# Ten of 544 weight steps with other matmul shapes and orders, and both halves of x in one tile

## The chip, the cores and the metric

The kernel runs on one core of a Trainium2 chip. The metric is the device time of one execution in microseconds, the median over runs. The core has five engines with queues of their own: TensorE (PE in the profile; its weight loads stand apart as PEld), VectorE (DVE), ScalarE (ACT), GpSimd (POOL) and SyncE (SP), which issues nearly all DMAs here.

## The reference

One inference step of a decoder layer on 256 prompt tokens and 8 sample tokens, 264 columns in all:

```
hn = RMSNorm(h);  P = hn @ W_in        # 4096 columns of hn, W_in cut into groups
A: sliding-window attention (12 heads of 128, window 128, sinks, ALiBi), times silu(z_a)
B: mLSTM matrix memory (6 heads), per-head RMS norm, sigmoid gate o_t, times silu(z_m)
C: chunked spatial gating (8 groups), times silu(z_c)
h = h + concat(A, B, C) @ W_out;  then a final RMSNorm
```

The two projections carry nearly all of the arithmetic. Everything is fp32. Beside y the step returns new rows of keys and values and the states of B and C.

## The kernel before

**Steps.** Activations stand transposed: 128 rows of the contraction on the partitions, the 264 tokens along the free axis, so x is 32 tiles k of 128 x 264. The weights are cut into 34 groups g of 512 output columns: 26 for W_in (`GROUPS`), then 8 for W_out (`NGO`). A group is done in 16 steps c, each with two tiles k (`KK = 2`): 34 x 16 = 544 steps (g, c), numbered n. A step's weights are one DMA of 512 KB (`load_w`, tile `wf`, 3 buffers, issued four steps ahead on SyncE's queue).

**Split into two.** Matmuls are in a shortened fp32 type (float32r), and precision comes from a split. For each step ScalarE writes the shortened weights `wh`, and VectorE writes the rest, `wl = wf - wh` (`split_w`, two steps ahead, 3 buffers each). x is split likewise into `xh` and `xl`, two tiles of 128 x 32 x 264 (`split_x` at the start, `split_y` for W_out). Each product is then three matmuls: `wh` with `xh`, `wh` with `xl`, `wl` with `xh`, each 128 x 128 weights by 264 columns.

**Order within a step.** For each of four blocks j of 128 output columns, for both k, the three matmuls go into the same PSUM bank; the four banks `mp` belong to the group. That is 4 x 2 x 3 = 24 matmuls a step, and six in a row into one bank:

```
for j in range(4):
    tick()
    out = main_ps[j][:, :T]
    for kk in range(KK):
        k = KK * c + kk
        s = slice(P * j, P * j + P)
        PE.matmul(out, wh[:, kk, s], xh[:, k], start=(k == 0), stop=False)
        PE.matmul(out, wh[:, kk, s], xl[:, k], start=False, stop=False)
        PE.matmul(out, wl[:, kk, s], xh[:, k], start=False, stop=(k == KT - 1))
    if c == NCH - 1:
        ...
            evac(g, kind, i, out)
```

**End of a group.** After step 15 `evac` empties a bank as soon as its j is done. For groups 8 and 9 (kind `mo`, the output gate of B) VectorE writes `et = mp * rstd`, and ScalarE later takes the sigmoid into `yb`. The next group writes the same four banks, so its first matmul into a bank waits until that bank has been read.

**Other work.** Attention and memory are generators. The recorder keeps a tally of the time that issued work should take (`clk`; 0.113 us for any float32r matmul, whatever its columns), and `tick()`, called before each j, resumes those generators that are due. So their small matmuls (transposes `mx<-sms`, scores `mx<-kT,aq`, products `mx<-pt,vtok`) stand between the blocks j of the weight steps; VectorE's and ScalarE's parts stand between the splits. Group 7 is the last of three for the attention queries, groups 8 to 10 are the gates `mo`; the heads' attention runs beside groups 6 to 8, that of the samples beside 8 and 9.

Every operation is recorded by one helper, so nearly all rows of the profile name its line, L201; tiles tell them apart.

Of the kernel before, what the change touches and what calls it, by code (L numbers as in the profile page):

```python
# [69 lines left out]
LAG = 6.0  # L70
NCH = KT // KK

SM = {}
# [15 lines left out]
def body(tc, xt, wi, wg, wo, sm, kc, vc, c0, wst, w00, bs, cgain, cbias,  # L89
# [3 lines left out]
    with ExitStack() as ctx:  # L93
# [30 lines left out]

        xh = cp.tile([P, KT, T], F32R, name="xh")
        xl = cp.tile([P, KT, T], F32R, name="xl")
        yb = cp.tile([P, KT, T], F32, name="yb")
# [32 lines left out]
        class Eng:  # L160
            """An engine whose issued work is tallied, so that dependent work is issued when due."""

# [95 lines left out]
        def rsqrt(out, x, scale, v, t):  # L258
            """out = (x * scale + EPS) ** -0.5, with one Newton step; v and t are scratch."""
            n = out.shape[0]  # L260
            V.tensor_scalar(v, x, -0.5 * scale, -0.5 * EPS, ALU.mult, ALU.add)
            A.activation(t, x, AF.Sqrt, scale=scale, bias=epsc[:n, 0:1])
            newton(out, v, t)
# [71 lines left out]

# [1 line left out]
        def gate_loads():  # L337
# [90 lines left out]

# [1 line left out]
        def head_loads(h):  # L430
# [150 lines left out]

# [1 line left out]
        def attn_kv(g):  # L583
# [140 lines left out]

# [1 line left out]
        def gmlp_prep():  # L726
# [80 lines left out]

# [1 line left out]
        def gated(kind, i, t):  # L809
# [142 lines left out]

# [1 line left out]
        def drain():  # L954
# [29 lines left out]
        for n, (g, c) in enumerate(steps):  # L984
# [16 lines left out]
            if g == NG and KK * c + KK > S_C:  # L1001
                while ("c", KK * c + KK - 1 - S_C) not in st:
                    tick(True)
            wh, wl = wh_t.pop(n), wl_t.pop(n)
            for j in range(4):
                tick()
                out = main_ps[j][:, :T]
                for kk in range(KK):
                    k = KK * c + kk
                    s = slice(P * j, P * j + P)  # L1010
                    PE.matmul(out, wh[:, kk, s], xh[:, k], start=(k == 0), stop=False)
                    PE.matmul(out, wh[:, kk, s], xl[:, k], start=False, stop=False)
                    PE.matmul(out, wl[:, kk, s], xh[:, k], start=False, stop=(k == KT - 1))
                if c == NCH - 1:
# [149 lines left out]
```

## Time and profile before

| | |
|---|---|
| two timed runs | 1715.74 and 1716.54 us, median 1716.14 |
| profiled execution, first to last instruction | 1715.0 us (no other time of that execution is recorded) |
| TensorE, matmuls | 1682.7 us (98%), 13754 records |
| TensorE, weight loads | 1664.7 us (97%), 13754 records |
| VectorE | 928.2 us (54%) |
| ScalarE | 733.2 us (43%) |
| GpSimd | 125.2 us (7%) |
| share of the chain that ended last | TensorE 94%, VectorE 3% |
| mean granted clock of TensorE | 0.994 |

A row of a group gives count, busy time and the mean of one. Matmuls and weight loads overlap, so their means are longer than the distance from one to the next; that distance is read from starts in the timeline, or from pieces of the chain that hold a count of matmuls.

### The profile page before, as it was taken

Reading aid. Unit: us, or ns where it says so; the run is one execution under the profiler, and the core shown is the slowest. Engines: PE = TensorE matmul, PEld = TensorE weight load, DVE = VectorE, ACT = ScalarE, POOL = GpSimd, SP = SyncE. Lnnn points to the kernel's source line nnn. Section 1 sums busy time; section 2 is a strip of 40 time slices with the busy share of each in tenths; the row PEclk is TensorE's granted clock in tenths of the full one; section 3 lists DMA queues with packets and bytes.
Section 4 is the critical chain, followed back from the end, with each engine's and each line's share of the span. In section 5 each row is a group of like instructions: output and inputs, shape, how many; then the busy total and the mean of one; then the engine's idle time right before and its main releaser. Section 6 shows DMA issues by size and latency. Waiting matters only on the chain.

```text
span 1715.0 us, 32547 instructions
## 1 busy us (share of the span) xinstructions
PE 1682.7 (98%) x13754; PEld 1664.7 (97%) x13754; DVE 928.2 (54%) x1262; ACT 733.2 (43%) x954; POOL 125.2 (7%) x113
## 2 busy tenths in 40 slices
PE   7999999999999999999999999999999999999995
PEld 7899999999999999999999999999999999999995
DVE  8755444555554455555655566444566554444445
ACT  4444433444444334344444444334454443444442
POOL 7300000000000000000101000000100030000002
PEclk9999999999999999999999999999999999999998
DMA  6566668555556666667677767666666666565663
GB/s 225 176 181 175 183 184 264 180 165 155 161 160 176 182 182 176 208 191 237 214 232 220 240 213 221 177 181 184 201 177 216 198 196 190 180 184 177 181 183 145
DMA packets 102178, 328.92 MB, mean 192 GB/s; under 512 B 11090, under 2 KB 24328, under 8 KB 102032
## 3 DMA queue, kind: packets, MB, share of 16 engines
q1 hardware_dynamic: 101072, 326.04, 62.7%
q8 instruction: 107, 1.75, 0.4%
q10 hardware_dynamic: 960, 0.81, 0.1%
q14 instruction: 39, 0.32, 0.1%
HBM read 314.20 MB, written 12.60 MB: 191 GB/s over the span
## 4 chain that ended last, share of the span: by engine, by line
PE 94%; DVE 3%; DMA 1%; issue 1%; ACT 0%; SPq 0%; DVEq 0%; ACTq 0%
PE mp L201 90%; PE mx L201 3%; DVE wl L201 1%; DVE xl L201 1%; DVE yb L201 1%; DMA wf<-wi 1%; DMA wf<-wo 1%; PE sn L201 0%; ACT wh L201 0%; PE gps L201 0%; DVE rstd L201 0%; DVE TM L201 0%; DVE mvs L201 0%; ACT L201 0%; DVE es L201 0%
## 5 line engine op out<-in xcount | busy, mean ns | idle before, releaser
L201 PE MATMUL mp<-xh,wl 128*128 128x264 f32 x4352 | 1240.6, 285 | 12.6 <-DVE wl L201 12.6
L201 PE MATMUL mp<-xh,wh 128*128 128x264 f32 x4352 | 1251.5, 288 | 0.6 <-ACT wh L201 0.6
L201 PE MATMUL mp<-xl,wh 128*128 128x264 f32 x4352 | 1238.2, 285 | 0.0
L201 DVE TENSOR_TENSOR wl<-wf,wh 128x1024 fp32r<-128x1024 f32 (+1 forms) x545 | 695.0, 1278 | 750.8 <-ACT wh L201 746.0
L201 ACT ACTIVATE wh<-wf 128x1024 fp32r<-128x1024 f32 (+1 forms) x545 | 575.0, 1058 | 839.1 <-PE mp L201 734.2
L201 PEld LDWEIGHTS mp<-xh,wl 128*128 128x128 f32 x4352 | 820.6, 189 | 15.2 <-DVE wl L201 15.0
L201 PEld LDWEIGHTS mp<-xh,wh 128*128 128x128 f32 x4352 | 820.7, 189 | 7.2 <-issue 5.0
L201 PEld LDWEIGHTS mp<-xl,wh 128*128 128x128 f32 x4352 | 820.8, 189 | 0.4
L201 POOL TENSOR_TENSOR acc<-acc,es 128x264 f32<-128x264 f32 x29 | 21.9, 754 | 417.1 <-ACT es L201 415.1
L201 POOL TENSOR_SCALAR_AFFINE_SELECT tmp<-bc 128x128 f32<-128x128 f32 x12 | 4.7, 412 | 496.6 <-DMA bc<-gd 496.6
L201 DVE SCALAR_TENSOR_TENSOR xl<-yb,sms,xh 128x264 fp32r<-128x264 f32 x32 | 35.1, 1135 | 1.2 <-ACT xh L201 1.1
L201 ACT ACT_TABLE_LOAD x25 | 32.1, 1283 | 3.4 <-DVE ar L201 2.2
L201 POOL MEMSET pad<- 128x1024 f32 x2 | 1.9, 950 | 406.4 <-PE mx L201 406.4
L201 POOL TENSOR_TENSOR acc<-acc,sq 128x528 f32<-128x528 f32 x15 | 24.0, 1603 | 1.2
L201 ACT ACTIVATE es<-et 128x264 f32<-128x264 f32 x36 | 14.0, 420 | 21.4 <-DVE yb L201 18.1
L201 POOL TENSOR_TENSOR cb<-cb,bc 128x2056 f32<-128x2056 f32 x6 | 21.7, 3616 | 0.0
L201 POOL TENSOR_TENSOR sq<-yb 128x528 f32<-128x528 f32 x15 | 20.6, 1375 | 9.8 <-DMA yb<-xt 9.1
L201 ACT ACTIVATE es<-yb 128x264 f32<-128x264 f32 x33 | 13.6, 412 | 16.3 <-DVE yb L201 16.3
L201 DVE TENSOR_TENSOR et<-mp,rstd 128x264 f32<-128x264 f32 x56 | 20.3, 423 | 0.0
L201 DVE SCALAR_TENSOR_TENSOR cb<-vb,wsk,cb 128x257 f32<-128x257 f32 x48 | 20.1, 480 | 0.0
L201 ACT ACTIVATE bias<-bias,ar 128x128 f32<-128x128 f32 (+1 forms) x24 | 10.7, 448 | 21.4 <-DVE ar L201 21.2
L201 ACT ACTIVATE xh<-yb 128x264 fp32r<-128x264 f32 x32 | 12.1, 412 | 17.7 <-DVE yb L201 17.7
(178 smaller groups left out, 471.6 us busy)
## 6 DMA issues: line engine op xcount, KB each, us to landing
wf<-wi SPq DMA_DIRECT2D x415, 512.0 KB, 3.6
wf<-wo SPq DMA_DIRECT2D x128, 512.0 KB, 3.6
cb<-c SPq DMA_DIRECT2D x12, 514.0 KB
o_cs<-cb SPq DMA_DIRECT2D x12, 514.0 KB, 6.4
vb<-vsd SPq DMA_DIRECT2D x12, 512.0 KB, 5.2
yb<-xt SPq DMA_DIRECT2D x34, 132.0 KB, 3.7
yb<-xt SPq DMA_DIRECT2D x15, 264.0 KB, 5.3
o_y<-yb SPq DMA_DIRECT2D x7, 528.0 KB, 3.1
```

What stands on the lines that cost most here:

```text
L201: return fn(*a, **k)
```

## The change

Nothing is removed from the arithmetic. `xh` and `xl` become two halves of one tile `xx`, in which row k holds `xh` and then `xl`, 264 columns each. Ten steps of groups 7, 8 and 9 are done in other shapes:

- **tail**, steps (7,6) and (7,7): each matmul is cut at column 256, into 256 and 8 columns.
- **halves**, steps (7,10) and (7,11): each is cut at 132.
- **banks**, steps (8,6) to (8,9): the same 24 matmuls, but j is the innermost loop, so each goes to another bank than the one before it. `tick()` is called once ahead of all 24 and four times behind.
- **wide**, steps (9,6) and (9,7): `wh` with 512 columns of a row of `xx` (all of xh and 248 of xl, into all 512 columns of the bank), `wh` with the last 16 columns of xl, `wl` with xh. At the end of group 9 ScalarE copies the bank's columns 264 to 511, VectorE adds them to columns 0 to 247, copies the other 16, and `evac` goes on from there. Both scratch rows, in `acc`, have one buffer.

```
+WIDE = 9
+SHAPES = {(7, 6): "tail", (7, 7): "tail", (7, 10): "halves", (7, 11): "halves", (8, 6): "banks", (8, 7): "banks",
+          (8, 8): "banks", (8, 9): "banks", (WIDE, 6): "wide", (WIDE, 7): "wide"}
...
-        xh = cp.tile([P, KT, T], F32R, name="xh")
-        xl = cp.tile([P, KT, T], F32R, name="xl")
+        xx = cp.tile([P, KT, 2, T], F32R, name="xx")
+        xh, xl = xx[:, :, 0], xx[:, :, 1]
...
             wh, wl = wh_t.pop(n), wl_t.pop(n)
+            shape = SHAPES.get((g, c), "plain")
+            if shape == "banks":
+                tick()
+                for kk in range(KK):
+                    k = KK * c + kk
+                    for w, x in ((wh, xh), (wh, xl), (wl, xh)):
+                        for j in range(4):
+                            PE.matmul(main_ps[j][:, :T], w[:, kk, P * j:P * j + P], x[:, k],
+                                      start=False, stop=False)
             for j in range(4):
                 tick()
                 out = main_ps[j][:, :T]
-                for kk in range(KK):
+                for kk in range(KK if shape != "banks" else 0):
                     k = KK * c + kk
                     s = slice(P * j, P * j + P)
-                    PE.matmul(out, wh[:, kk, s], xh[:, k], start=(k == 0), stop=False)
-                    PE.matmul(out, wh[:, kk, s], xl[:, k], start=False, stop=False)
-                    PE.matmul(out, wl[:, kk, s], xh[:, k], start=False, stop=(k == KT - 1))
+                    if shape == "wide":
+                        pair = xx[:, k].rearrange("p a t -> p (a t)")
+                        PE.matmul(main_ps[j][:, :512], wh[:, kk, s], pair[:, :512], start=False, stop=False,
+                                  skip_group_check=True)
+                        PE.matmul(out[:, 248:], wh[:, kk, s], xl[:, k, 248:], start=False, stop=False)
+                        PE.matmul(out, wl[:, kk, s], xh[:, k], start=False, stop=False)
+                        continue
+                    cuts = {"plain": (0, T), "tail": (0, 256, T), "halves": (0, 132, T)}[shape]
+                    for w, x, first, last_ in ((wh, xh, True, False), (wh, xl, False, False), (wl, xh, False, True)):
+                        for a, b in zip(cuts, cuts[1:]):
+                            PE.matmul(out[:, a:b], w[:, kk, s], x[:, k, a:b], start=(first and k == 0),
+                                      stop=(last_ and k == KT - 1))
+                if c == NCH - 1 and g == WIDE:
+                    add, mix = acc[:, 0, :248], acc[:, 1]
+                    A.activation(add, main_ps[j][:, T:512], AF.Copy)
+                    tt(V, mix[:, :248], add, out[:, :248], ALU.add)
+                    V.tensor_copy(mix[:, 248:], out[:, 248:])
+                    out = mix
```

What this does to the order of instructions, at three places. First TensorE at step (7,6), the first block j (`mp` is the block's bank, the last number the columns). Before:

```order
L201 MATMUL mx<-sms,bias 128x128 x3
L201 MATMUL mp<-xh,wh 128x264
L201 MATMUL mp<-xl,wh 128x264
L201 MATMUL mp<-xh,wl 128x264
L201 MATMUL mp<-xh,wh 128x264
L201 MATMUL mp<-xl,wh 128x264
L201 MATMUL mp<-xh,wl 128x264
```

And with the change (the helper's line is now L204, and both halves of x read xx):

```order
L204 MATMUL mx<-sms,bias 128x128 x3
L204 MATMUL mp<-xx,wh 128x256
L204 MATMUL mp<-xx,wh 128x8
L204 MATMUL mp<-xx,wh 128x256
L204 MATMUL mp<-xx,wh 128x8
L204 MATMUL mp<-xx,wl 128x256
L204 MATMUL mp<-xx,wl 128x8
L204 MATMUL mp<-xx,wh 128x256
L204 MATMUL mp<-xx,wh 128x8
L204 MATMUL mp<-xx,wh 128x256
L204 MATMUL mp<-xx,wh 128x8
L204 MATMUL mp<-xx,wl 128x256
```

Each matmul has become two with the same weights, and each row has a weight load of its own; steps (7,10) and (7,11) look the same with 132 twice.

Second, TensorE at step (9,6), where the six matmuls of a block were as above. Two plain ones end step (9,5), then come both k of the first block:

```order
L204 MATMUL mp<-xx,wh 128x264 x2
L204 MATMUL mp<-xx,wl 128x264
L204 MATMUL mp<-xx,wh 128x512
L204 MATMUL mp<-xx,wh 128x16
L204 MATMUL mp<-xx,wl 128x264
L204 MATMUL mp<-xx,wh 128x512
L204 MATMUL mp<-xx,wh 128x16
L204 MATMUL mp<-xx,wl 128x264
```

The count stays, the columns are 512, 16 and 264 in place of three times 264.

Third, VectorE at the end of group 9, behind the last products of the samples' attention (`yb`, `pnb`) and nine splits. Before:

```order
L201 TENSOR_TENSOR yb<-yb,pnb 128x3x8
L201 TENSOR_TENSOR pnb<-pnb,mx 128x24
L201 TENSOR_TENSOR yb<-yb,pnb 128x3x8
L201 TENSOR_TENSOR wl<-wf,wh 128x1024 x9
L201 TENSOR_TENSOR et<-mp,rstd 128x264 x4
L201 TENSOR_TENSOR wl<-wf,wh 128x1024 x16
```

With the change, in place of the four `et<-mp,rstd`, and ahead of the same sixteen splits:

```order
L204 TENSOR_TENSOR acc<-acc,mp 128x248
L204 COPY acc<-mp 128x16
L204 TENSOR_TENSOR et<-acc,rstd 128x264
L204 TENSOR_TENSOR acc<-acc,mp 128x248
L204 COPY acc<-mp 128x16
L204 TENSOR_TENSOR et<-acc,rstd 128x264
L204 TENSOR_TENSOR acc<-acc,mp 128x248
L204 COPY acc<-mp 128x16
L204 TENSOR_TENSOR et<-acc,rstd 128x264
L204 TENSOR_TENSOR acc<-acc,mp 128x248
L204 COPY acc<-mp 128x16
L204 TENSOR_TENSOR et<-acc,rstd 128x264
```

Four instructions have become twelve; each add also waits for ScalarE's copy of that bank. Outside groups 7 to 10 no engine's order changes, and on SyncE and GpSimd none changes anywhere.

## The prediction

> **What bounds the kernel now.** I read the page's first two parts and its chain, then the chain in order of time, then single loads and matmuls in the timeline, because the change is about the price of single matmuls.
>
> ```profile
> span 1715.0 us, 32547 instructions
> PE 1682.7 (98%) x13754; PEld 1664.7 (97%) x13754; DVE 928.2 (54%) x1262; ACT 733.2 (43%) x954; POOL 125.2 (7%) x113
> ...
> PEclk9999999999999999999999999999999999999998
> ...
> PE 94%; DVE 3%; DMA 1%; issue 1%; ACT 0%; SPq 0%; DVEq 0%; ACTq 0%
> ...
> L201 PE MATMUL mp<-xh,wl 128*128 128x264 f32 x4352 | 1240.6, 285 | 12.6 <-DVE wl L201 12.6
> L201 PE MATMUL mp<-xh,wh 128*128 128x264 f32 x4352 | 1251.5, 288 | 0.6 <-ACT wh L201 0.6
> L201 PE MATMUL mp<-xl,wh 128*128 128x264 f32 x4352 | 1238.2, 285 | 0.0
> ```
>
> TensorE is busy for 98% of the span, carries 94% of the chain that ended last, and waits 13 us in all for the split weights. The 285 ns of one matmul are no price: matmuls overlap. The price is the distance between starts, and the chain in order of time gives it in its two long pieces of main matmuls (start, length, what; the first and last row are for later):
>
> ```profile
> 25.08 2.26 DVE wl L201
> ...
> 219.88 46.86 PE mp L201 x384
> ...
> 495.38 265.09 PE mp L201 x2172
> ...
> 1366.11 9.07 DMA wf<-wo
> ```
>
> 46.86 us for 384 is 122.0 ns each, 265.09 for 2172 (from group 9 on) is 122.1. So a weight step of 24 costs 2.93 us, and 544 steps 1593 us. Counted in matmuls, the ten changed steps lie between 385 and 500 us, on this path: what a matmul there costs more, the kernel pays.
>
> How much of 122 ns is columns, and how much is weights? Two stretches ran at half clock (in the rows by window the third number from the end is the granted clock; then two starts from the timeline):
>
> ```profile
> 27.60:31.00 3.40, 3.40 (x17) 3.40 (x17) 3.40 (x3) 0.45 (x2) 2.04 (x2) 0.51 0.73 214
> ...
> 1379.40:1382.70 3.30, 3.30 (x17) 3.30 (x16) 3.30 (x2) 0.00 (x0) 3.22 (x2) 0.50 0.55 161
> ...
> 1380.14 0.42 PE L201 MATMUL mp<-xh,wh 128*128 128x264 f32 x1
> 1380.36 0.42 PE L201 MATMUL mp<-xl,wh 128*128 128x264 f32 x1
> ```
>
> There 264 columns take 220 ns, 0.833 ns a column, so 110 ns at the full clock; 12 of the 122 ns are something else. Each matmul also has a weight load of its own (13754 of both on the page). What a load costs when the matmul before it is too short to hide it shows once, behind four transposes of six columns:
>
> ```profile
> 159.53 0.32 PEld L201 LDWEIGHTS mx<-sms,R 6*128 6x128 f32 x4
> 159.87 0.19 PEld L201 LDWEIGHTS mp<-xh,wh 128*128 128x128 f32 x1
> 159.98 0.19 PEld L201 LDWEIGHTS mp<-xl,wh 128*128 128x128 f32 x1
> 160.10 0.19 PEld L201 LDWEIGHTS mp<-xh,wl 128*128 128x128 f32 x1
> ...
> L201 PEld LDWEIGHTS mx<-sms,R 6*128 6x128 f32 x4 | 0.3, 137 | 0.1
> ```
>
> The main weights' next load starts 110 ns after the one before (159.87 to 159.98), though only six columns stood ahead of it; behind a matmul of 264 columns the distance is 120 again. The transposes' own loads follow at (0.32 - 0.137) / 3 = 61 ns, but one of those takes 137 ns and one of the main weights 189, so they are a cheaper kind.
>
> **The change part by part.**
>
> *Tail (two steps, 48 old matmuls).* 264 columns become 256 and 8, each with its own load. The 8 cost a load: 110 ns, or 61 (as the transposes), or 122 (no better than now). The 256 cost between a load's 110 and 122; I take 118, the columns' 107 plus the 12. Per old matmul +106 ns (50 to 122), in all **+5.1 us** (2.4 to 5.9). I take 110 since it is the row of these same weights.
>
> *Halves (two steps, 48).* 132 columns are 55 ns, under any load, so each half costs a load: 2 x 110 - 122 = +98 ns (0 to 122), **+4.7 us** (0 to 5.9).
>
> A rule of the Trainium skill says otherwise: in "TensorE: Matmul & The Clock Gate", Back-to-back issue gap, a stream of load and matmul pairs is given at about 81 ns for 128 columns and 131 for 512. By it, as an estimate, tail would be +2.7 us, halves +1.9 and wide -0.5, a total of some 1721 us. This trace does not agree: between those two figures 264 columns would stand near 100 ns, and they take 122.
>
> *Wide (two steps, 16 pairs of j and kk).* Three matmuls of 264 (366 ns) become 512, 16 and 264 columns. No row has 512 columns: by 0.417 ns each they are 213, by 122 x 512 / 264 they are 237; I take 225 (213 + 12). The 16 cost a load, 110 (61 to 122). 225 + 110 + 122 - 366 = +91 ns (30 to 115), **+1.5 us** (0.5 to 1.8). The wide matmul saves one of three loads, but loads were hidden, and the 16-column rest exposes one.
>
> *The end of group 9.* Four times ScalarE now copies 248 columns, VectorE adds, copies 16 columns and only then multiplies by rstd; the next group's matmuls wait for the 16-column copy to free the bank.
>
> ```profile
> 521.99 1.23 DVE L201 TENSOR_TENSOR wl<-wf,wh 128x1024 fp32r<-128x1024 f32 x1 [1.67 <-ACT wh L201]
> 523.13 1.45 DVE L201 TENSOR_TENSOR et<-mp,rstd 128x264 f32<-128x264 f32 x4
> 524.91 1.23 DVE L201 TENSOR_TENSOR wl<-wf,wh 128x1024 fp32r<-128x1024 f32 x1 [0.33 <-ACT wh L201]
> ...
> L201 DVE COPY qs<-aq 128x8 f32<-128x8 f32 x12 | 2.1, 172 | 0.4
> ...
> L201 ACT ACTIVATE yb<-et 128x264 f32<-128x264 f32 x12 | 4.1, 410 | 0.0
> ```
>
> Now VectorE empties four banks in 1.45 us, beginning at 523.1, when its split is done; TensorE reaches the first bank of group 10 at about 523.7 and the others 0.73 us apart (6 x 122 ns). With the change one bank takes 0.36 + 0.17 + 0.36 = 0.9 us of VectorE (0.42 for ScalarE's copy of the next bank lies beside it, since it waits only for the add before). So 0.9 against 0.73: the first bank is free about on time, the other three come 0.17 late each, with handovers **+0.7 us**. Bounds: 0, and 2.4 if the copies lie in the chain too (1.4 - 0.73 per bank for three, and 0.4). Behind VectorE's waiting adds stands the split of step (10,2), behind ScalarE's copies its wh: some 2 to 3 us late, and not needed until 6 us after the group's start.
>
> *Banks (four steps, 96 matmuls).* Same matmuls, same loads; each goes to another bank than the one before. Before, every sixth does, inside the 46.86 us above, at no visible price: **0**. Bounds: the 12 ns vanish or double, -1.2 to +1.2 us.
>
> *Attention work moves.* The recorder counts 0.113 us for any main matmul, so it places transposes and scores of the heads up to two steps earlier; in step (8,6) the scores of two heads stand back to back behind all 24 matmuls. What the second of them waits for, the product of an earlier head, was issued before, with the step's 2.9 us to cover it. **0**; if that cover were gone, one such product:
>
> ```profile
> L201 DVE TENSOR_TENSOR yb<-yb,mx 128x256 f32<-128x256 f32 x12 | 4.9, 416 | 1.1 <-PE mx L201 1.1
> ```
>
> 0.4 us. SyncE's queue (all loads of weights) and GpSimd keep their order.
>
> *One tile for x.* This touches all 544 steps. Their times repeat every four steps, read off the splits, each of which starts when a step frees its buffer:
>
> ```profile
> 539.61 1.22 DVE L201 TENSOR_TENSOR wl<-wf,wh 128x1024 fp32r<-128x1024 f32 x1 [1.75 <-ACT wh L201]
> 542.52 1.23 DVE L201 TENSOR_TENSOR wl<-wf,wh 128x1024 fp32r<-128x1024 f32 x1 [1.69 <-ACT wh L201]
> 545.42 1.23 DVE L201 TENSOR_TENSOR wl<-wf,wh 128x1024 fp32r<-128x1024 f32 x1 [1.67 <-ACT wh L201]
> 548.34 1.22 DVE L201 TENSOR_TENSOR wl<-wf,wh 128x1024 fp32r<-128x1024 f32 x1 [1.69 <-ACT wh L201]
> 551.32 1.23 DVE L201 TENSOR_TENSOR wl<-wf,wh 128x1024 fp32r<-128x1024 f32 x1 [1.76 <-ACT wh L201]
> ```
>
> 2.91, 2.90, 2.92, 2.98 us. The weight buffers go round in three, so it isn't they; a row of x is 1056 bytes, 4 x 256 + 32, so its place within 256 bytes repeats after eight k, which is four steps. I think this place is what changes the step. In the new tile xh moves on by 2112 bytes (8 x 256 + 64): it meets four of the eight places and xl the other four, one of each old step's two. The mean over the places stays, so **0**. Bounds: all steps at 2.90, -0.028 x 544 = -15 us; all at 2.98, +0.052 x 544 = +28 us.
>
> **Sum.** 5.1 + 4.7 + 1.5 + 0.7 = +12.0 us, 1727.0 of span. The timed runs lie 0.7 to 1.5 us above that span, their median 1.1, which covers what lies around it: **1728.1 us**. Without the tile the bounds add up to +1.7 and +17.6, so 1718 to 1734.
>
> **The rivals.**
>
> *Loads are cheap behind short matmuls* (61 ns): 2.4 + 0 + 0.5 + 0.7 = +3.6, 1720 us. For it, the transposes; against it, the 110 ns of the main weights' own row.
>
> *The clock drops in the short steps.* With 8 or 132 columns to a load the array streams columns for about half the time. Tail and halves last 10.9 and 10.6 us by the sum; at half clock throughout they would last twice that, 1750 us, for half of it 1739. Against it: while weight steps run, half clock appears in those two stretches only, each just behind a wait of TensorE (the chain's rows at 25.08 and 1366.11 us), never in busy ones. The Trainium skill's page "TensorE: Matmul & The Clock Gate", under A second HAM failure mode: psum-queue depth-cycling, reports a kernel whose clock swung because it cycled through PSUM banks with small idle spells; by it the banks steps too could go at 220 ns, and this trace, with a bank change every sixth matmul, shows no such swing.
>
> *x is read more slowly in the new tile, everywhere*: the place of xl, now always 32 bytes past a multiple of 64, costs as in the worst step. +28 + 12 = 1757 us, over 2% slower. It decides from a mean step of 2.97 us ((34.3 - 12) / 544 = 0.041 above 2.93). For it, the 2.98; against it, that all eight places still occur.
>
> *x is read faster everywhere*: -15 + 12, 1713 us. The same rows, the other end.
>
> **How the numbers follow.** Forecast 0.70; cheap loads 0.10; clock 0.07; tile slower 0.07; tile faster 0.06. The range 1716 to 1740 holds the first two, the milder half of the clock's case and a shift of the tile's of some us: it leaves out about 0.15. Two per cent, 34 us, is about what a measurement of this kernel can tell from no change. Slower by more needs the tile's worst case or the clock's at its full length: 0.06. Faster by more would need all bounds at once: 0.01. Within: 0.93.
>
> **What would show it.** Right: in the tail steps starts some 118 and 110 ns apart, in the halves 110 and 110, so 5.4 to 5.5 us a step; wide 3.66 us a step; banks 2.93 us; TensorE stopped three times by about 0.2 us at the start of group 10; a clock of 1.00 from 375 to 545 us; plain steps of 2.93 us on the mean, in a cycle of two steps if the place of x makes it. Wrong, first of all: a mean plain step that has moved by more than 0.01 us, since that is multiplied by 534, or loads at 61 ns.

## The result, and the profile after

The changed kernel takes 1729.88 us (two runs, 1729.25 and 1730.52), the kernel before 1716.14. The ratio is 1.0083 [1.0067, 1.0100]: 0.8% longer, inside the 2% called no change, and within 2 us of the forecast 1728.1.

The first parts of the page of the changed kernel, its chain that ended last, and its two main groups of matmuls:

```profile
span 1728.8 us, 32757 instructions
PE 1696.6 (98%) x13850; PEld 1676.7 (97%) x13850; DVE 930.6 (54%) x1270; ACT 735.2 (43%) x958; POOL 127.1 (7%) x113
...
PEclk9999999999999999999999999999999999999998
...
PE 93%; DVE 3%; DMA 1%; issue 1%; ACT 1%; SPq 0%; DVEq 0%; ACTq 0%
...
L204 PE MATMUL mp<-xx,wh 128*128 128x264 f32 (+2 forms) x8768 | 1617.7, 286 | 1.5 <-DVE et L204 0.7
...
L204 PE MATMUL mp<-xx,wl 128*128 128x264 f32 (+1 forms) x4384 | 1245.2, 286 | 11.6 <-DVE wl L204 11.4
```

TensorE still carries all of it: 98% busy, 93% of the chain, 96 matmuls more (13754 to 13850: four steps of 24), the full clock but for three short pieces at the start (below). TensorE's busy time has grown by 13.9 us and the span by 13.8. What is new is an idle time of 0.7 us behind VectorE's `et`, which the prediction did not have.

The starts on TensorE's timeline price the new shapes (start, length, and the columns at the end of the shape; one row can stand for several matmuls in a row). First steps (7,6), (7,11) and (9,6):

```profile
394.20 0.37 PE L204 MATMUL mp<-xx,wl 128*128 128x256 f32 x2
394.43 0.60 PE L204 MATMUL mp<-xx,wh 128*128 128x256 f32 x4
394.89 0.37 PE L204 MATMUL mp<-xx,wl 128*128 128x256 f32 x2
...
412.22 0.39 PE L204 MATMUL mp<-xx,wl 128*128 128x132 f32 x2
412.45 0.61 PE L204 MATMUL mp<-xx,wh 128*128 128x132 f32 x4
412.89 0.27 PE L204 MATMUL mp<-xx,wl 128*128 128x132 f32 x1
...
506.15 0.41 PE L204 MATMUL mp<-xx,wh 128*128 128x512 f32 x2
506.41 0.37 PE L204 MATMUL mp<-xx,wl 128*128 128x264 f32 x1
506.62 0.41 PE L204 MATMUL mp<-xx,wh 128*128 128x512 f32 x2
```

From 394.20 to 394.89 stand six matmuls, three pairs of 256 and 8 columns: 0.69 us, 230 ns a pair (the sum had 118 + 110). From 412.22 to 412.89 stand six of 132 columns: 0.67 us, 111.7 ns each (the sum had 110). From 506.15 to 506.62 stand 512, 16 and 264 columns: 0.47 us (the sum had 0.457). Over whole steps, read from the first main matmul of one step to that of the next:

| step | before us | after us | part of the change |
|---|---|---|---|
| (7,6), (7,7) | 4.765, 3.101 | 7.481, 5.523 | tail, +5.14 together |
| all of group 7 | | | +10.04, so halves +4.9 |
| (8,8), (8,9) | 2.981, 3.159 | 2.924, 2.901 | banks; attention's matmuls moved out of (8,9) |
| (8,15) | 2.935 | 3.771 | the new idle time |
| (9,6), (9,7) | 3.015, 2.919 | 3.834, 3.736 | wide, +1.64 together |
| (10,0) | 2.986 | 4.011 | the end of group 9, +1.03 |

The end of group 9, on VectorE and ScalarE (an idle time of an engine before a row, and what ended it, stands in brackets):

```profile
536.56 0.41 DVE L204 TENSOR_TENSOR acc<-acc,mp 128x248 f32<-128x248 f32 x1
536.88 0.17 DVE L204 COPY acc<-mp 128x16 f32<-128x16 f32 x1
537.09 0.43 DVE L204 TENSOR_TENSOR et<-acc,rstd 128x264 f32<-128x264 f32 x1
537.62 0.41 DVE L204 TENSOR_TENSOR acc<-acc,mp 128x248 f32<-128x248 f32 x1
538.69 0.41 DVE L204 TENSOR_TENSOR acc<-acc,mp 128x248 f32<-128x248 f32 x1
...
538.13 0.38 ACT L204 ACTIVATE acc<-mp 128x248 f32<-128x248 f32 x1 [0.69 <-DVE acc L204]
```

VectorE begins a bank every 1.07 us (536.56, 537.62, 538.69), not every 0.90. ScalarE's copy for the third bank starts at 538.13, 0.1 us after VectorE's add of the second has ended (537.62 + 0.41 = 538.03), and ends at 538.51, just in front of the third add: by these times it is in the chain after all. 1.07 - 0.73 = 0.34 us late on each of three banks, 1.02 us.

The idle time at (8,15), in the chain that ended last, in order of time (start, length, what); the last row is the long plain piece from the start of group 10 on:

```profile
478.71 4.50 PE mp L204 x36
483.21 0.18 ACT r L204
483.39 0.96 ACT wh L204
...
484.38 1.09 DVE wl L204
...
485.52 0.43 DVE et L204
...
540.40 234.81 PE mp L204 x1920
```

TensorE still works through step (8,15), but the chain has left it at 483.21: what decides when group 9 can begin is ScalarE's `r` (a part of the samples' softmax), then ScalarE's and VectorE's halves of a split, and only then `et`, which empties the banks. TensorE stands still for the last 0.7 us of this. In the plain piece matmuls are 234.81 / 1920 = 122.3 ns apart, where they were 122.1.

Where the 13.8 us of span came in: the start of each group's first main matmul, after minus before, read from both traces, and the same for four of the experiments (us): the new tile alone (tile_only), the old tiles with the new shapes (old_tiles), the banks steps left plain (no_banks) and the banks of group 9 let go first (early_release).

| kernel | g 1 | g 7 | g 8 | g 9 | g 10 | g 11 | g 27 | g 28 | g 33 |
|---|---|---|---|---|---|---|---|---|---|
| changed | 0.83 | 1.05 | 11.09 | 11.79 | 13.46 | 14.55 | 15.36 | 13.50 | 13.76 |
| tile_only | 0.28 | 0.54 | 0.56 | 0.47 | 0.51 | 0.54 | 1.23 | 0.80 | 1.03 |
| old_tiles | -0.33 | -0.41 | 9.69 | 10.43 | 10.41 | 10.41 | 10.33 | 8.88 | 8.87 |
| no_banks | -0.49 | -0.27 | 9.77 | 9.68 | 11.35 | 12.46 | 13.29 | 11.32 | 11.63 |
| early_release | 0.74 | 1.00 | 11.04 | 11.75 | 13.41 | 13.52 | 14.36 | 14.62 | 14.94 |

Two columns are not shown to have anything to do with the change: the start (column g 1), and group 27, where TensorE waits for a load of weights that is slow in every kernel (8.4 us in the changed one, 9.9 before, against 3.6 in the median). At both places the clock falls to half for pieces of 3.4 us that stand elsewhere in each execution. The rows by window of the changed kernel (granted clock third from the end):

```profile
18.90:22.30 3.40, 3.40 (x18) 0.50 0.67 232
29.10:32.50 3.40, 3.40 (x17) 0.50 0.59 210
56.40:59.80 3.40, 3.40 (x22) 0.50 0.61 218
...
1379.30:1382.70 3.40, 3.40 (x30) 1.00 0.73 229
```

Before had one such piece at 27.6 and one at 1379.4; the changed kernel has three at the start and none behind the slow load. There it gains 1.86 us: the piece of before cost some 1.7 us (half of 3.4), and its waits in group 27 were 2.1 us long against 1.4, together somewhat more than the gain. At the start the pieces do not explain the +0.83 us: early_release, the same work up to there, has its only piece at 7.5 us and yet +0.74, and no_banks has -0.49. Kernels with the two old tiles scatter there from -0.61 (the run with placed weights below) to +0.79 (the one with x moved by 128 bytes). So both are of the size of the scatter of single runs. The Trainium skill, in "TensorE: Matmul & The Clock Gate", What's actually happening, gives a free-running activity window of about 3.4 us and calls the phase at the start variable; the 3.40 us here agree.

### The profile page after: what moved, and what is told of

It is laid out like the page before. It is cut to its first block, busy times and chain, and to the rows that moved or that the text cites. A ratio compares the mean times of both kernels' runs of the same rounds, so it can differ in the third digit from the quotient of the medians.

```text
span 1728.8 us, 32757 instructions
## 1 busy us (share of the span) xinstructions
PE 1696.6 (98%) x13850; PEld 1676.7 (97%) x13850; DVE 930.6 (54%) x1270; ACT 735.2 (43%) x958; POOL 127.1 (7%) x113
## 4 chain that ended last, share of the span: by engine, by line
PE 93%; DVE 3%; DMA 1%; issue 1%; ACT 1%; SPq 0%; DVEq 0%; ACTq 0%
PE mp L204 90%; PE mx L204 3%; DVE wl L204 1%; DVE yb L204 1%; DMA wf<-wo 1%; DVE xx L204 1%; DMA wf<-wi 1%; PE sn L204 0%; ACT wh L204 0%; DMA yb<-xt 0%; PE gps L204 0%; DVE rstd L204 0%; DVE TM L204 0%; ACT es L204 0%; DVE mvs L204 0%
## 5 line engine op out<-in xcount | busy, mean ns | idle before, releaser
L204 PE MATMUL mp<-xx,wh 128*128 128x264 f32 (+2 forms) x8768 | 1617.7, 286 | 1.5 <-DVE et L204 0.7
L204 PEld LDWEIGHTS mp<-xx,wh 128*128 128x128 f32 x8768 | 1359.0, 189 | 9.5 <-issue 6.9
L204 PE MATMUL mp<-xx,wl 128*128 128x264 f32 (+1 forms) x4384 | 1245.2, 286 | 11.6 <-DVE wl L204 11.4
L204 DVE TENSOR_TENSOR wl<-wf,wh 128x1024 fp32r<-128x1024 f32 (+1 forms) x545 | 692.6, 1274 | 758.9 <-ACT wh L204 747.3
L204 ACT ACTIVATE wh<-wf 128x1024 fp32r<-128x1024 f32 (+1 forms) x545 | 574.9, 1057 | 846.1 <-PE mp L204 750.4
L204 PEld LDWEIGHTS mp<-xx,wl 128*128 128x128 f32 x4384 | 823.6, 189 | 14.9 <-DVE wl L204 14.1
L204 POOL TENSOR_TENSOR acc<-acc,es 128x264 f32<-128x264 f32 x29 | 21.9, 754 | 417.0 <-ACT es L204 414.9
L204 POOL TENSOR_SCALAR_AFFINE_SELECT tmp<-bc 128x128 f32<-128x128 f32 x12 | 4.4, 389 | 498.7 <-DMA bc<-gd 498.7
L204 DVE SCALAR_TENSOR_TENSOR xx<-yb,sms,xx 128x264 fp32r<-128x264 f32 x32 | 33.5, 1084 | 1.4 <-ACT xx L204 1.4
L204 POOL MEMSET pad<- 128x1024 f32 x2 | 1.9, 950 | 414.3 <-PE mx L204 414.3
L204 POOL TENSOR_TENSOR acc<-acc,sq 128x528 f32<-128x528 f32 x15 | 25.6, 1708 | 1.2
L204 ACT ACTIVATE es<-et 128x264 f32<-128x264 f32 x36 | 13.9, 420 | 21.3 <-DVE yb L204 18.0
L204 POOL TENSOR_TENSOR cb<-cb,bc 128x2056 f32<-128x2056 f32 x6 | 22.6, 3770 | 0.0
L204 ACT ACTIVATE es<-yb 128x264 f32<-128x264 f32 x33 | 13.6, 412 | 16.4 <-DVE yb L204 16.3
L204 POOL TENSOR_TENSOR sq<-yb 128x528 f32<-128x528 f32 x15 | 19.7, 1316 | 10.6 <-DMA yb<-xt 10.1
L204 DVE SCALAR_TENSOR_TENSOR cb<-vb,wsk,cb 128x257 f32<-128x257 f32 x48 | 20.0, 480 | 0.0
L204 ACT ACTIVATE xx<-yb 128x264 fp32r<-128x264 f32 x32 | 12.0, 412 | 17.8 <-DVE yb L204 17.8
L204 ACT ACTIVATE bias<-bias,ar 128x128 f32<-128x128 f32 (+1 forms) x24 | 10.7, 448 | 19.3 <-DVE ar L204 19.1
L204 DVE TENSOR_TENSOR et<-mp,rstd 128x264 f32<-128x264 f32 x52 | 18.8, 423 | 0.0
L204 ACT ACTIVATE yb<-yb,sms 128x264 f32<-128x264 f32 x32 | 16.5, 517 | 1.0
L204 POOL TENSOR_SCALAR_AFFINE_SELECT wm<-wm 128x1024 f32<-128x1024 f32 x1 | 1.1, 1097 | 194.1 <-DMA wm<-wst 194.1
```

The source lines that it names most:

```text
L204: return fn(*a, **k)
```

## The experiments

**The new tile alone.** The changed kernel with an empty table of shapes, and so without the new end of group 9:

```
-SHAPES = {(7, 6): "tail", ...
+SHAPES = {}
```

> Only the one tile for x; all 544 steps keep their old shapes. Place theory (where a row of x stands within 256 bytes sets the step): plain steps of 2.929 and 2.931 us in a cycle of two, against 2.98, 2.91, 2.90, 2.92 in a cycle of four; 534 to 544 times +0.0015 us, so about 1717 us. Rival (the joined tile adds waits of its own, as the first group of the changed kernel, 0.83 us longer, could mean): the same cycle, but 1718 us or more, with the loss at the start, where x is split.

Measured: 1718.11 us (10 runs) against 1716.33 (13 runs), 1.0010 [1.0000, 1.0019]. The steps are 2.928 and 2.932 us in turn, a cycle of two, where before had 2.982, 2.911, 2.902 and 2.919 in a cycle of four. So the tile costs about 1 us in all (+1.03 at group 33 in the table), and the cycle follows the layout of x. The total is one that the rival named too (1718 us or more), but its loss at the start is not there: 0.28 us in this trace, while 0.95 us come in from group 1 to group 27, little by little.

**The old tiles with the new shapes,** without wide, which needs the one tile:

```
-        xx = cp.tile([P, KT, 2, T], F32R, name="xx")
-        xh, xl = xx[:, :, 0], xx[:, :, 1]
+        xh = cp.tile([P, KT, T], F32R, name="xh")
+        xl = cp.tile([P, KT, T], F32R, name="xl")
```

> Two tiles for x as before; tail, halves and banks, no wide (and so no longer end of group 9). Theory (each part is paid where it stands): tail +5.1, halves +4.9, the stall at the end of group 8 +0.8, so 1727 us, with plain steps still in the cycle of four. Rival (the tile carries part of the loss): 1726 us or less.

Measured: 1725.69 us (4 runs), 1.0054 [1.0037, 1.0071]. Group 7 costs 10.10 us here and 10.04 in the changed kernel, group 8 0.74 and 0.71; beyond that nothing drifts. The total is below the theory's 1727 us, on the rival's side; in the trace the missing part lies at the start (-0.33 us) and in group 27 (-1.45), the two places of scatter, and not where the tile would act. Tail and halves do not need the tile, and the idle time of group 8 is not the tile's.

**The banks steps left plain,** with all else as changed:

```
-SHAPES = {..., (8, 6): "banks", (8, 7): "banks", (8, 8): "banks", (8, 9): "banks", ...
+SHAPES = {...
```

> The changed kernel with steps (8,6) to (8,9) plain again. Theory (the calls of tick behind the 24 matmuls push the samples' attention to the end of group 8, and the wait for its chain there costs 0.8 us): TensorE goes through step (8,15) in 2.9 us, total 0.8 us less than the changed kernel. Rival (the moves of group 7 cause it): step (8,15) still at 3.8 us. The banks steps' own price: theory 0, so nothing more changes.

Measured: 1728.35 us (one run, before 1715.31 beside it). Step (8,15) lasts 2.935 us as before, and group 8 now costs -0.09 us in place of +0.71. The shapes of group 7 are still there, so the rival falls. ScalarE's timeline around that place, in the changed kernel

```profile
479.46 1.06 ACT L204 ACTIVATE wh<-wf 128x1024 fp32r<-128x1024 f32 x1 [4.15 <-PE mp L204]
482.71 0.40 ACT L204 ACTIVATE Ls<-Ls,r 128x129 f32<-128x129 f32 x1 [2.19 <-DVE r L204]
...
483.30 1.04 ACT L204 ACTIVATE wh<-wf 128x1024 fp32r<-128x1024 f32 x1
```

and in the run without banks:

```profile
479.68 0.41 ACT L204 ACTIVATE Ls<-Ls,r 128x129 f32<-128x129 f32 x1 [2.75 <-DVE r L204]
...
481.16 1.06 ACT L204 ACTIVATE wh<-wf 128x1024 fp32r<-128x1024 f32 x1 [0.80 <-ACT r L204]
```

TensorE does the samples' scores at the same time in both (from 476.4 and 476.6 us). But in the changed kernel one more split stands ahead of the softmax in ScalarE's and VectorE's queues: that split's `wh` could only be made at 479.46, when TensorE let a buffer go. VectorE's first parts of the softmax stood behind its `wl`, so ScalarE's part `Ls` waited for them until 482.71; the next `wh` came at 483.30, and VectorE's next `wl` and then `et` behind that. Without banks the softmax goes first. So the cost of the banks steps is not in their matmuls; it is their calls of `tick()`, which put attention's work at another place in two other queues.

**The banks of group 9 let go first.** VectorE's adds and copies of all four banks come before the four products with rstd, each into an `et` of its own, and ScalarE's copies use both scratch rows in turn:

```
-                    add, mix = acc[:, 0, :248], acc[:, 1]
+                    add, mix = acc[:, j % 2, :248], hp.tile([P, T], F32, name="et", bufs=4)
...
+                    mixes.append(mix)
+                    if j == 3:
+                        for jj, mix in enumerate(mixes):
+                            kind, i, _ = GROUPS[g][jj]
+                            tt(V, mix, mix, rstd, ALU.mult)
+                            spawn(gated(kind, i, mix), urgent)
```

> The changed kernel, but at the end of group 9 VectorE does all four adds and copies before the four multiplications by rstd, into separate tiles, and ScalarE's copies have two buffers. Theory (TensorE waits at the start of group 10 because VectorE needs about 1 us a bank against TensorE's 0.73): 0.6 us a bank now, so step (10,0) falls from 4.01 to about 3.0 to 3.1 us, total 1 us less. Rival (ScalarE's copies set the pace): step (10,0) stays above 3.5 us.

Measured: 1731.66 us (one run). VectorE's timeline:

```profile
537.42 0.41 DVE L204 TENSOR_TENSOR et<-acc,mp 128x248 f32<-128x248 f32 x1
...
537.84 0.40 DVE L204 TENSOR_TENSOR et<-acc,mp 128x248 f32<-128x248 f32 x1
```

A bank now takes 0.42 us here (537.42 to 537.84) and at most 0.50, less than TensorE's 0.73, and step (10,0) falls from 4.011 to 3.022 us: the group costs 0.11 us in the table (13.41 to 13.52) in place of 1.09. The 1.0 us were the late banks. The run changes the order of VectorE's work and the copies' scratch rows at once, so it does not tell what each is worth. The total shows none of it, since this execution has a piece of half clock at 1393 us, behind the slow load, and so does not gain the 1.86 us of the changed kernel there (14.36 to 14.62): a single run does not resolve 1 us.

**Is a price of 111 ns the load's?** Groups 28 to 33, in which nothing else runs, with another shape each, steps 1 to 14 (`narrow`: 64 of each block's 128 columns of weights, the other half left out):

```
+    SHAPES[28, _c] = "halves" if _c < 8 else "sixths"
+    SHAPES[29, _c] = "thirds" if _c < 8 else "cut232"
+    SHAPES[30, _c] = "tail" if _c < 8 else "plain"
+    SHAPES[31, _c] = "banks"
+    SHAPES[32, _c] = "narrow"
+    SHAPES[33, _c] = "narrow_halves"
```

> One tile for x; all groups plain except those of W_out, whose steps 1 to 14 are: group 28 halves (steps 1 to 7) and sixths of 44 columns (8 to 14), group 29 thirds of 88 and then 232+32, group 30 tail and then plain, group 31 banks, group 32 weights of 64 columns only (half of each block's rows left out), group 33 the same in halves of 132. Theory (a matmul too short to hide the next weight load costs that load, 111 ns for 128 weight columns, whatever its own columns): 223 ns for a pair of halves, 333 for thirds, 666 for sixths, 223 for 232+32, 230 for tail; weights of 64 columns load in about half, so halves of those cost about 2 x 57 to 62 ns, and 264 columns drop from 122 towards 112. Sum about 1889 us. Rival A (111 ns is a price of each matmul, not of its load): the same for halves, thirds and sixths, but 2 x 111 with 64 weight columns too, and 264 columns stay at 122. Rival B (banks helped by going round): banks steps below 2.90 us; theory 2.93.

Measured: 2081.55 us (one run) in place of some 1889, since the clock halved in two of the groups, which was not expected. Rows by window (us, TensorE's busy time and records, then the granted clock), for halves, for sixths, for thirds (and the first cuts at 232), for the other cuts at 232 and for halves of narrow weights:

```profile
1418.30:1450.40 32.10, 32.10 (x290) 1.00 0.38 119
1477.10:1661.40 184.30, 184.30 (x865) 0.50 0.06 18
1681.50:1783.90 102.40, 102.40 (x482) 0.50 0.12 36
1783.90:1845.40 61.50, 61.50 (x291) 0.50 0.17 52
...
2013.50:2052.10 38.60, 38.60 (x627) 1.00 0.50 152
```

Halves cost 111.6 ns a matmul, tail 230 a pair. With 64 columns of weights, halves cost 61.9 ns a matmul and 264 columns 120.6: the 111 are not a price of any matmul but of its weights. Banks alternate at 2.913 and 2.960 us a step, 2.937 on the mean where plain steps have 2.930: no price. The new fact is the clock. The sixths (44 columns) ran at 111 to 112 ns for some 40 matmuls, then at 213 ns at half clock; the thirds (88 columns) did so after 3.6 us; and the cuts at 232 behind them stayed at half clock, also 213 ns a matmul, until 2 us into the plain steps.

**Where the clock drops.** The same groups with other shapes: halves for even k and thirds for odd k; halves alone; thirds of narrow weights; sixths of narrow weights:

```
+    SHAPES[28, _c] = "mixed"
+    SHAPES[30, _c] = "halves"
+    SHAPES[32, _c] = "narrow_thirds"
+    SHAPES[33, _c] = "narrow_sixths"
```

> As the ladder, steps 1 to 14 of four groups of W_out: group 28 k by turns in halves and in thirds (mean 106 columns to a load), group 30 halves, group 32 weights of 64 columns with thirds of 88 columns, group 33 the same with sixths of 44 (half of each block's rows left out in 32 and 33). Clock theory (the clock halves where columns fill too little of the time): in the ladder 33% of columns halved it within 4 us, 48% never did; so group 30 (49%) stays at 111 to 112 ns a matmul for all of 78 us, and group 28 (39%) tells on which side it falls: 111 ns if it holds, 213 ns if not. Rival (it halves after some time of loads without cover, whatever the columns): group 30 falls to 213 ns too. Weights of 64 columns: if 62 ns were their load, thirds and sixths cost 62 ns a matmul as well; if it was the 132 columns (55 ns and some), thirds fall to about 45 and sixths to about 30 ns.

Measured: 1996.27 us (one run). The four in that order:

```profile
1421.20:1508.30 87.10, 87.10 (x782) 1.00 0.28 82
1566.50:1636.10 69.60, 69.60 (x626) 1.00 0.37 108
1693.10:1747.70 54.60, 54.60 (x940) 1.00 0.47 137
1779.10:1963.40 184.30, 184.30 (x1730) 0.50 0.09 24
```

Take 0.417 ns a column against the distance of matmuls (111.7, 111.6, 58.3 and 106.7 ns from steps of 60, 48, 72 and 144). Mixed (105.6 columns on the mean) has its columns for 39% of the time, halves 49%, narrow thirds 63%, and all hold the full clock for as long as they last. Narrow sixths have 18.3 of some 58 ns, 31%, and fall to half; the thirds above had 36.7 of 111, 33%, and fell. So with 128 columns of weights the limit lies between 33 and 39%, and the runs with 64 (31 and 63%) agree with that; halves of the changed kernel, at 49%, were on the safe side of it. That holds for falling only: the cuts at 232 had columns for 52% of the time (110 of 213 ns) and did not bring the clock back. Counted as columns per time, one limit would fit both: narrow sixths 0.75 a ns, thirds 0.79 (both fell), cuts at 232 at half clock 0.62 (stayed low), mixed 0.95, halves 1.18 (held). Which of the two the clock follows was not tested. The price of a load follows too: 111.7 ns for 128 columns of weights and 58.3 for 64 are 0.83 ns a column and 5 ns. At half clock 213.3 and 106.7 ns are 1.67 a column, twice as much, and nothing on top.

**What sets the cycle of four steps?** First x moved with everything behind it, by 128 unused bytes; then x by 16 bytes within tiles made larger, so that the tiles behind moved by other amounts; then all that lies behind x by 128, the weights among it, x where it was. Places below are the address of row k of x less that of the weights' row for the same k, modulo 256:

```
+        gap = cp.tile([P, 32], F32, name="gap")          # ahead of x: both move
...
-        xh = cp.tile([P, KT, T], F32R, name="xh")        # 16 bytes, xl likewise
+        xh = cp.tile([P, KT * T + 4], F32R, name="xh")[:, 4:].rearrange("p (k t) -> p k t", t=T)
...
+        gap = cp.tile([P, 32], F32, name="gap")          # behind x: the weights move
```

> The kernel before with 128 unused bytes ahead of xh and xl, so that each row of x stands where the row four tiles (two steps) later stood. Place theory: the step of 2.98 us moves from c = 0, 4, 8, 12 to c = 2, 6, 10, 14; total unchanged, 1716. Rival (the cycle comes from the number of the step, or from its loads): it stays at c = 4, 8, 12.

Measured: 1716.29 us. The long step stays at c = 0, 4, 8, 12. The place of x alone, my step in the prediction, is not the cause.

> The kernel before with both halves of x moved by 16 bytes within tiles of their own. Place theory: a cycle of four steps stays, its times may differ, mean between 2.90 and 2.98 us (1701 to 1744 us in all). Rival (place plays no part): exactly the steps of before, 2.98, 2.91, 2.90, 2.92.

Measured: 1720.26 us, steps of 2.940, 2.947, 2.939 and 2.914 us, 2.935 on the mean. Against the weights xh moved by 48 bytes here and xl by 16: all four lengths changed.

> The kernel before with 128 unused bytes behind xh and xl: x stands where it stood, the split weights 128 bytes further (with both moved by 128 bytes the cycle of four steps had not changed). Theory (what sets the step is where a row of x stands relative to the weights that are loaded beside it): the step of 2.98 us moves from c = 4, 8, 12 to c = 2, 6, 10, 14, total still about 1716 us. Rival (the number of the step sets it, places do not): 2.98 us stays at c = 4, 8, 12.

Measured: 1716.69 us (before 1717.08 beside it). VectorE's splits, whose distances are the steps, for the same steps as in the prediction's rows:

```profile
539.48 1.23 DVE L202 TENSOR_TENSOR wl<-wf,wh 128x1024 fp32r<-128x1024 f32 x1 [1.67 <-ACT wh L202]
542.40 1.22 DVE L202 TENSOR_TENSOR wl<-wf,wh 128x1024 fp32r<-128x1024 f32 x1 [1.69 <-ACT wh L202]
545.38 1.22 DVE L202 TENSOR_TENSOR wl<-wf,wh 128x1024 fp32r<-128x1024 f32 x1 [1.76 <-ACT wh L202]
```

2.92 and 2.98 us, where before had 2.91 and 2.90. From matmul to matmul the steps are 2.902, 2.919, 2.982 and 2.911 us from c = 0 on, those of before moved by two, as 128 of 256 bytes should move them. The place of a row of x relative to the weights loaded beside it sets the step.

**Placing the weights.** If that is so, the place can be chosen. The kernel before, the buffers of `wh` and `wl` a little larger (a small tile was put into another's buffer to make room), and the weights put into them at an offset by step, so that a row of x lies 224 bytes (even k) and 0 bytes (odd k) past its weights modulo 256 in every step, as before only in each fourth:

```
+            def place(raw, first):
+                o = ((160 + 64 * c - first - WB * ((-n) % 3)) % 256) // 4
+                return raw[:, o:o + KK * 512].rearrange("p (k e) -> p k e", k=KK)
-            hi = wp.tile([P, KK, 512], F32R, name="wh")
+            hi = place(wp.tile([P, WB // 4], F32R, name="wh"), WH0)
...
```

> The kernel before in all its shapes and orders, x in its two tiles; only the place of the split weights in their buffers is chosen anew for each step, so that a row of x lies 224 bytes (even k) and 0 bytes (odd k) past the weights loaded beside it, counted modulo 256, in every step, as it does in the kernel before in the steps c = 2, 6, 10, 14 only, those of 2.902 us. Theory (the place of a row of x relative to the weights loaded beside it sets a step's length): all steps last 2.90 us, the mean falls from 2.928 to 2.902 us, 544 x 0.026 = 14 us, so 1702 us (1700 to 1705) and no cycle of four steps is left. Rival 1 (the cycle of four comes from the step's number, or from the place of x together with something else that the larger buffers don't move): the four lengths 2.982, 2.911, 2.902 and 2.919 us stay, 1716 us (1714 to 1719). Rival 2 (the cycle has a fixed sum that is only handed round, as in the weights moved by 128 bytes, where the mean stayed): all steps alike at 2.928 us, 1716 us without a cycle.

Measured: 1707.51 us (5 runs) against 1716.36 (9 runs), 0.9949 [0.9935, 0.9963]. The cycle of four is gone. VectorE's splits:

```profile
533.36 1.23 DVE L203 TENSOR_TENSOR wl<-wf,wh 128x1024 fp32r<-128x1024 f32 x1 [1.68 <-ACT wh L203]
536.27 1.23 DVE L203 TENSOR_TENSOR wl<-wf,wh 128x1024 fp32r<-128x1024 f32 x1 [1.68 <-ACT wh L203]
```

All plain steps last 2.908 us, where the theory had 2.902; the gain is 9 of the expected 14 us, about two thirds.

**All eight places,** another in each of eleven groups:

```
+PLACE = dict(zip((10, 11, 12, 13, 22, 23, 24, 29), range(0, 256, 32)))
+PLACE.update({3: 96, 4: 160, 5: 32})
```

> As the run with chosen places, but the place is another in eleven groups: for groups 10, 11, 12, 13, 22, 23, 24 and 29 a row of x lies 0, 32, 64, 96, 128, 160, 192 and 224 bytes (even k; 32 more for odd k) past the weights loaded beside it in all 16 steps, for groups 3, 4 and 5 it is 96, 160 and 32, and 224 in all others. Theory (each step's length is set by its own place): all steps of a group are alike; 96 gives 2.98 us (groups 3 and 13), 160 gives 2.91 (groups 4 and 23), 32 gives 2.92 (groups 5 and 11), 224 gives 2.91 (group 29); the four places that the kernel before never has lie between their neighbours, 2.91 to 2.95, and the places below 2.90 that a better version would need are not there. Rival (a step is long because the place has jumped from the step before, and costs nothing where it stays): all eleven groups at 2.91 us a step. The sum by the theory is 2 groups x 16 x 0.07 us + 1 to 2 us more than 1707, 1711 us; by the rival 1707 us; both within the scatter of single runs, so the steps decide and not the time.

Measured: 1711.98 us (one run). Steps by place (even k; odd k 32 more), all steps of a group alike but for the first few:

| place | 0 | 32 | 64 | 96 | 128 | 160 | 192 | 224 |
|---|---|---|---|---|---|---|---|---|
| us a step | 2.922 | 2.915, 2.928 | 2.922 | 2.988, 2.988 | 2.942 | 2.922, 2.922 | 2.895 | 2.908 |

Two numbers are the two groups of one place. Splits in group 13 (place 96):

```profile
685.59 1.23 DVE L206 TENSOR_TENSOR wl<-wf,wh 128x1024 fp32r<-128x1024 f32 x1 [1.76 <-ACT wh L206]
688.58 1.23 DVE L206 TENSOR_TENSOR wl<-wf,wh 128x1024 fp32r<-128x1024 f32 x1 [1.76 <-ACT wh L206]
```

2.99 us in every step but the first two, without any jump of the place between them: the rival falls. The theory missed two things: it denied a place below 2.90, and 192 has 2.895; and it gave 160 the 2.91 of the kernel before, where 2.922 came. That the two groups at 32 differ by 13 ns says that the place is not all of it.

**The best place everywhere,** 192 (even k) and 224 (odd k) in all 544 steps; the line before is that of the run with 224 and 0, and the buffers begin 32 bytes lower here:

```
-                o = ((160 + 64 * c - first - WB * ((-n) % 3)) % 256) // 4
+                o = ((-32 + 64 * c - first - WB * ((-n) % 3)) % 256) // 4
```

> The kernel before in all its shapes and orders, the split weights placed so that a row of x lies 192 bytes (even k) and 224 bytes (odd k) past the weights loaded beside it in all 544 steps: the place whose steps lasted 2.895 us in group 24 of the sweep. Theory (the place alone sets the length of a step, in every group): 2.895 us a step instead of 2.908 with chosen places (0 bytes for odd k), 544 x 0.013 = 7 us less than its 1707.5, so 1700.5 us (1698 to 1703), 0.9% below the kernel before. Rival (group 24 was short for another reason than its place, such as what stands around it): steps of 2.91 us and 1707 us.

Measured: 1705.14 us (5 runs) against 1716.80 (9 runs), 0.9931 [0.9918, 0.9945]: the lowest time of all, 0.7% below the kernel before (inside the 2% called no change, but clear of 1.0) and 25 us below the changed one. From the run with 224 it is not clear by time, since the two intervals overlap; the steps tell them apart. VectorE's splits at the end of a group and behind it:

```profile
563.36 1.23 DVE L204 TENSOR_TENSOR wl<-wf,wh 128x1024 fp32r<-128x1024 f32 x1 [1.67 <-ACT wh L204]
566.25 1.22 DVE L204 TENSOR_TENSOR wl<-wf,wh 128x1024 fp32r<-128x1024 f32 x1 [1.67 <-ACT wh L204]
...
569.15 1.23 DVE L204 TENSOR_TENSOR wl<-wf,wh 128x1024 fp32r<-128x1024 f32 x1 [0.31 <-ACT wh L204]
572.13 1.23 DVE L204 TENSOR_TENSOR wl<-wf,wh 128x1024 fp32r<-128x1024 f32 x1 [1.75 <-ACT wh L204]
575.11 1.23 DVE L204 TENSOR_TENSOR wl<-wf,wh 128x1024 fp32r<-128x1024 f32 x1 [1.75 <-ACT wh L204]
577.93 1.23 DVE L204 TENSOR_TENSOR wl<-wf,wh 128x1024 fp32r<-128x1024 f32 x1 [1.60 <-ACT wh L204]
```

The settled steps are the theory's 2.895 us (566.25 - 563.36 = 2.89), yet the total is 4.6 us above its 1700.5. Part of that is seen: behind each change of group or piece of attention the step takes three steps to settle (2.98, 2.98 and 2.82 us by the splits from 569.15 on, 2.980, 2.927 and 2.880 from matmul to matmul), and in groups with attention many steps never do. A plain group gains 0.45 us over before, one with other work beside it 0 to 0.4. Against the run with 224 a plain group gains 0.17 us of the 0.21 that 16 x 0.013 would give, and groups 15 to 20, with other work in them, nothing. Why a disturbed stream takes two or three steps to come back to the short length was not tried.

## Why the prediction was right, and where it was off

Every term of its sum, against what the traces show (us):

| term | predicted | measured |
|---|---|---|
| tail | +5.1 | +5.14 |
| halves | +4.7 | +4.9 |
| wide | +1.5 | +1.64 |
| end of group 9 | +0.7 | +1.03 |
| banks' matmuls | 0 | about 0 |
| attention moved | 0, at most 0.4 | +0.84 in (8,15), group 8 in all +0.71 |
| one tile for x | 0 | about +1.0 (drift of groups 1 to 6 and 11 to 26) |
| start, and the wait at 1379 us | not in the sum | +0.83, -1.86 |
| sum | +12.0 | +13.8 (some 0.4 in small rests) |

- **The load as the floor of a short matmul**: right. The one pair of load rows behind the six-column transposes gave 110 ns, the runs 111.7. The run with 64 columns of weights shows that it is the weights: 61.9 ns with the same 132 columns of x. Rival "cheap loads" is refuted for 128 x 128 weights.
- **Wide**: the mechanism was right, the price 102 ns for each pair of j and kk in place of 91: 468 ns by the step, so the 457 were 11 short. The 512 columns and their 16 are together 346, not 335.
- **End of group 9**: the step that failed is the sentence that ScalarE's copy "lies beside" VectorE's work. It may start only behind the add of the bank before, and its 0.38 us and two handovers outlast the 16-column copy and the product (0.17 + 0.43 of overlapping rows). 0.34 us late per bank in place of 0.17. Freeing all four banks first, with two scratch rows for the copies, took the 1.0 us away; that the copies alone set the pace is read from the times of the rows, and no run changed them alone.
- **Attention moves, 0**: the step that failed. It looked at products on TensorE and VectorE in the banks steps themselves, with a cover of 2.9 us, and at one product of 0.4 us if the cover went. What moved was the order of a split and the softmax of the samples in (8,15), six steps behind the last banks step, in ScalarE's and VectorE's queues, ahead of the `et` that frees the banks. The prediction looked at the order of these queues at the end of group 9 only, not of group 8. The run without banks takes the idle time away.
- **One tile, 0**: the time held (2.930 us for 2.928), and so did the cycle of two steps. Its reason held by half: the place counts modulo 256 bytes, but relative to the weights, not in itself. The bounds were real ones: 2.895 and 2.988 us a step, as the sweep has them, are -18 and +33 us over 544 steps.
- **The clock rival**: rightly unlikely here (full clock from 59.8 to 1715 us), but no fantasy. With columns for a third of the time it came within 4 us; the changed kernel's halves have columns for 49% of the time, its tail steps for 48%.
- **Luck**: the mechanisms of tail, halves and wide were right, and they are 11.7 of the 13.8 us. That the total also came so near owes something to chance: attention, the tile and the end of group 9 cost some 2 us more than the sum had, and the start and the wait in group 27, which it did not have, took 1.0 us back.

The Trainium skill's rule in "TensorE: Matmul & The Clock Gate", Back-to-back issue gap (81 ns for 128 columns, 131 for 512) does not hold here: 132 columns took 111.7 ns, and 264 already 122. What the Trainium skill reports on the same page, under A second HAM failure mode: psum-queue depth-cycling, is not seen either: fourteen steps of bank changes at every matmul kept the full clock at 2.937 us a step.

## What to carry to other kernels

Price a matmul as the longer of its columns and its own weight load, and read the load from a place in the trace where short matmuls leave it bare; then measure what comes on top (264 columns take 110 ns by the half-clock rows, and 122 here). Cutting columns below that floor only multiplies loads, and cutting them to a third of the load's time halved the clock as well. When an edit moves the call that interleaves other work, compare the order on every engine up to the next point where a buffer is handed over, not only in the edited steps. A cycle in the lengths of equal steps is a lead: here it was a matter of where two operands lie relative to each other, and choosing that place saved 12 us, while every shape that changed the time cost some.

## What the runs showed of the hardware that I had not expected

- The granted clock halves with TensorE busy without a gap, if its matmuls have columns for 33% of the time or less; at 39% and more it stays. It came 3.6 to 6.3 us after the first such matmul and stayed for as long as they went on (up to 212 us). Once there, matmuls with columns for 52% of the time did not bring it back; plain ones did within some 5 us.
- A weight load costs 0.83 ns for each column of weights and 5 ns (58.3 for 64, 111.7 for 128); at half clock it is 1.67 ns a column alone (106.7 and 213.3).
- The length of a step of 24 matmuls depends on where the row of x lies relative to the weights loaded beside it, modulo 256 bytes: 2.895 to 2.988 us, 3%. What in the chip makes the place matter, no run shows.
- Behind a disturbance the short steps take two or three steps to return. Why was not settled, nor why one place gave 2.915 us in one group and 2.928 in another.
